# A hybrid decoder trunk in float32 on one core: the second low half of the first x block is queued without waiting for the low half of the weights

## Chip, cores and metric

The kernel runs on one core of one Trainium2 chip. The metric is the device time of one execution in microseconds (us). Lower is better.

## What is computed

The reference is a trunk with one attention layer and a final norm (the convolution layer has a weight of its own, but with a depth of one it is not reached). All of it is float32. Cut to what matters:

```python
D_MODEL = 4096; SEQ = 256; N_HEADS = 32; HEAD_DIM = 128
xn = rms_norm(x, norm_attn)                      # (256, 4096)
q, k, v, g = split(xn @ w_in_attn, 4)            # w_in_attn: (4096, 16384)
# strictly causal stick-breaking attention, head by head (log space, suffix sums)
A[t,s] = sigmoid(z_ts) * prod_{s<j<t} (1 - sigmoid(z_tj)),  s < t
o = A @ v
h = x + (o * silu(g)) @ w_out_attn               # w_out_attn: (4096, 4096)
return rms_norm(h, final_norm)
```

So there are two large products: 256 rows of x by a matrix of 4096 x 16384, and 256 rows of the gated heads by one of 4096 x 4096.

## The kernel before

**Products in three parts.** A float32 operand is split into a high part, which the tensor engine takes exactly (type fp32r), and a low part, the remainder. A product is then three matmuls that add up in one PSUM bank: high by high and two cross terms, in the names of the trace `wh,sh` (high weights, high x), `wl,sh` (low weights, high x) and `wh,sl` (high weights, low x). ScalarE (ACT) makes the high parts by a cast (`wh<-raw`), VectorE (DVE) the low ones by a subtraction (`wl<-raw,wh`). In the second large product the names of the left side are `oh` and `ol`.

**Units, steps and parts.** The work is a list of *units*: 16 over the columns of the first matrix (u = 0 to 15), then 4 over those of the second. A unit has 16 *steps* over the contracted dimension, and a step brings two tiles of weights (`raw`, 128 partitions by 1024 numbers, two transfers of 256 KB). In unit 0 a step is eight products, four on each tile, so 24 matmuls of 128x512; in the other units some steps get by with seven products, by sums and differences of blocks made on VectorE, and by an accumulating transfer on GpSimd's queue. Each unit writes PSUM banks b1 to b7. While unit u+1 multiplies, the attention of unit u's two heads runs between its matmuls. The very first tile of weights alone is cut into its two halves of 512 columns (c = 0 and 1), so that the first products can start earlier.

**x.** For unit 0 the left side comes from x transposed: step i takes block i, 256 columns of x by 256 rows, that is a pair of chunks c = 0 and 1 of 128 columns, each 128 partitions by 256 numbers. `blocks_of(i)` loads it (`xs`), multiplies it by the gain of the norm and makes the high and low parts (`sh`, `sl`). For i > 0 ACT scales and casts the whole pair. For i = 0 VectorE does it, chunk by chunk: `sh` of chunk c, then `sl` of chunk c. Afterwards the block is scaled in place on ACT (two ACTIVATEs) and differences of its quarters are made on VectorE, for the units that come later.

**What sets the order.** All engine work is emitted by a planner, class `Plan`, that runs a small event simulation while the program is built. Work is a set of generators. A generator asks for an engine (`nc.work`), waits for a name that another tells (`nc.until`, `nc.tell`), or takes a buffer of a ring (`nc.take`). When an engine of the simulation becomes free, the waiting request with the smallest key is emitted next: `key` is the time at which its product is due. What is emitted stays in that order on its engine (`keep_in_program_order`), and on the chip each engine takes its instructions in that order. The waits of the simulation are not waits on the chip: there an instruction waits only for the data and the buffers that it needs. So a line of the kernel that waits in the simulation moves instructions, and every later decision of the planner follows from the times of the earlier ones.

The places that the rest speaks of:

- `piece(n, c, ...)` makes high and low part of a tile or a half of one, and tells `("low", n, k)` once the low part of columns k is there. Part n = 0 is the first tile of step 0, n = 1 the second one, n = 2 and 3 the tiles of step 1, and so on.
- `products()` walks the list of products, and each asks for `("low", n, c)` and for the form of x that it uses.
- The last unit computes output columns 3072 to 4095 (blocks 6 and 7 of 512), as two row tiles t = 0 and 1. Its last five parts do their products bank by bank, `LAST_ORDER = (5, 4, 2, 3)`. Banks b5 and b4 complete row tile t = 1, and banks b2 and b3 complete t = 0. `block_done` adds a bank to `h`, `part_done` has ACT square and sum it, `finish` makes the factor of the final norm for all 128 rows of a tile, and `rows_out` scales the eight blocks of that tile and has SyncE (SP) issue their eight transfers to `out_dram`, 256 KB each.

Of the kernel before, what the change touches and what calls it, by code (L numbers as in the profile page):

```python
# [248 lines left out]
def kernel(  # L249
# [10 lines left out]
    nc = Plan(tc)  # L260
# [14 lines left out]
    def minus(out_, full, part):  # L275
        nc.vector.tensor_tensor(out=out_, in0=full, in1=part.bitcast(F32), op=ALU.subtract)
# [45 lines left out]
    def place_at(u, s):  # L322

        return place_of[u + int(s // NS), step_at(u + int(s // NS), int(s % NS))]
# [5 lines left out]
    def dve(emit, n, key=None, more=0, **kw):  # L330
        n = n if isinstance(n, tuple) else (n,)
        cost = sum(vector_ns(m) for m in n) + 122 * (len(n) - 1) + more
        return nc.work("vector", cost, emit, soon() if key is None else key, **kw)

    def act(emit, n, key=None, **kw):
        n = n if isinstance(n, tuple) else (n,)
        cost = sum(scalar_ns(m) for m in n) + 100 * (len(n) - 1)
        return nc.work("scalar", cost, emit, soon() if key is None else key, **kw)
# [14 lines left out]
    def moved(engine, emit, sizes, key, after=None, hold=False, adds=False, wait=0):  # L353
        issue = 550 if engine == "gpsimd" else 330
        return nc.work(
            engine, issue * len(sizes), emit, key, after=after, hold=hold, moves=[(4 * P * n, adds) for n in sizes],
            wait=wait,
        )
# [149 lines left out]
    def new_forms(i, what):  # L508
        n = len(SEVEN_FORMS if i in (SEVEN if what == "s" else SEVEN_OUT) else EIGHT_FORMS)
        h = sp.tile([P, n, P], F32R, tag=f"xh{i}", name=f"{what}h{i}")  # L510
        l = sp.tile([P, n, P], F32R, tag=f"xl{i}", name=f"{what}l{i}")
        forms[i] = h, l
        return h, l
# [18 lines left out]
    def sums_of(i, y, what, key):  # L532

        tt = nc.vector.tensor_tensor
        if i not in (SEVEN if what == "n" else SEVEN_OUT):
            yield from differences(i, y, key)
        else:

            def four():
                tt(out=y[:, 0, :], in0=y[:, 1, :], in1=y[:, 0, :], op=ALU.subtract)  # L540
                tt(out=y[:, 1, :], in0=y[:, 3, :], in1=y[:, 1, :], op=ALU.subtract)
                tt(out=y[:, 3, :], in0=y[:, 0, :], in1=y[:, 3, :], op=ALU.subtract)
                tt(out=y[:, 2, :], in0=y[:, 2, :], in1=y[:, 3, :], op=ALU.add)

            yield dve(four, (P, P, P, P), key)
            yield from both_parts(i, slice(4, 7), y[:, 1:4, :], key)

            yield nc.until(("used", 0 if what == "n" else OUT0, i))
            yield from both_parts(i, slice(1, 2), y[:, 0:1, :], key)
        nc.tell(("form", what, i))  # L550

    def blocks_of(i):

        key = place_of[0, i]
        tag = ("one", "two", "s", "s")[i % 4]
        yield nc.take(tag)
        pool, inside, bufs = (wp, "s", SINGLES) if tag == "s" else (ap, tag, 1)
        y = pool.tile([P, KT, S], F32, tag=inside, name=f"xs{i}", bufs=bufs)
        y4 = y.rearrange("p k (a b) -> p (k a) b", a=NT)
        h, l = new_forms(i, "s")  # L560
        gain = lambda c: gcol[:, i * KT + c : i * KT + c + 1]
        if i:
            yield moved(
                "sync", lambda: nc.sync.dma_start(y, xT[i]), [KT * S], key - 1, hold=True, wait=1300 * i - 600 if i < 4 else 0
            )

            def scaled():
                for c in range(KT):
                    nc.scalar.activation(y[:, c, :], y[:, c, :], AF.Copy, scale=gain(c))
                nc.scalar.copy(h[:, 0:4, :], y4)  # L570

            yield act(scaled, (S, S, 2 * S), key - 2e3)
            yield dve(lambda: minus(l[:, 0:4, :], y4, h[:, 0:4, :]), 2 * S, key)
        else:
            yield moved("scalar", lambda: nc.scalar.dma_start(gcol, gain_in), [KC], key - 1)
            yield moved("scalar", lambda: nc.scalar.dma_start(y, xT[i]), [KT * S], key - 1, hold=True)
            for c in range(KT):
                hc, lc = (t[:, 2 * c : 2 * c + 2, :].rearrange("p a b -> p (a b)") for t in (h, l))

                yield dve(  # L580
                    lambda: nc.vector.tensor_scalar(out=hc, in0=y[:, c, :], scalar1=gain(c), scalar2=None, op0=ALU.mult),
                    S, key - 1,
                )
                nc.tell(("sh", c))
                yield nc.until(("low", 0, c))
                yield dve(
                    lambda: nc.vector.scalar_tensor_tensor(
                        out=lc, in0=y[:, c, :], scalar=gain(c), in1=hc.bitcast(F32), op0=ALU.mult, op1=ALU.subtract
                    ),
                    S, key - 1,  # L590
                )
        nc.tell(("form", "s", i))
        later = place_at(0, i + BLOCKS_LATER)
        if not i:

            def scaled():
                for c in range(KT):
                    nc.scalar.activation(y[:, c, :], y[:, c, :], AF.Copy, scale=gain(c))

            yield act(scaled, (S, S), later)  # L600
        yield from sums_of(i, y4, "n", later)
        nc.give(tag)


    def blocks_all():
        for i in range(1, NS):
            if i > 3:
                yield nc.until(("used", 0, i - 4))
            nc.start(blocks_of(i))

    together(blocks_of(0), load(), blocks_all())
    nc.run(1e3)
    warm = att.tile([P, W], F32, tag="att", name="warm")
# [723 lines left out]
```

## Time and profile before

| | |
|---|---|
| time, median of 3 runs | 1693.47 us (1693.3 to 1694.87) |
| the profiled execution's own time | 1693.27 us |
| its span in the profile | 1691.6 us |
| busy share of the span | PE 99%, weight loads 84%, DVE 95%, ACT 71%, GpSimd 19% |
| granted TensorE clock | 0.997 |
| HBM read and written | 403 MB and 8 MB, 243 GB/s over the span |

The profile counts its times from the start of the span. PE is the tensor engine's matmuls, PEld its weight loads, DVE is VectorE, ACT is ScalarE, SPq is the queue of SyncE, which issues most transfers. A row of the timeline gives the start, the duration, engine, line and operation, out<-in, the shape and a count, and in square brackets how long the engine sat idle before it and what ended that. All instructions stand on L132, the line of the recording helper, so they are told apart by the names of their tiles. Matmuls overlap: one of 128x512 is listed with some 0.38 us, while the next starts 0.22 us after it.

### The profile page before, as it was taken

The page shows a single profiled execution, that of the slowest core. Times are in us where ns is not written, and L with a number is a line of the kernel's source. Part 1 is how long each engine was busy: PE and PEld are TensorE (multiplying, and loading weights), DVE is VectorE, ACT ScalarE, POOL GpSimd, SP SyncE. Part 2 cuts the span into 40 slices and gives each one's busy share as a digit, 9 for nine tenths or more (in the row PEclk, how much of TensorE's full clock was granted, in tenths as well). Part 3 has the DMA queues.
Part 4 walks back from the last instruction along what each step waited for, and adds up shares of the span by engine and source line. Part 5 has one row for each costly group of instructions (what it writes and reads, how often), then busy time and mean ns, then how long its engine had stood idle before and what let it go on. Part 6 is the DMA issues. An engine that isn't in the chain of part 4 may idle for free.

```text
span 1691.6 us, 25185 instructions
## 1 busy us (share of the span) xinstructions
PE 1674.7 (99%) x7776; PEld 1418.6 (84%) x7776; DVE 1600.5 (95%) x2025; ACT 1202.2 (71%) x1665; POOL 325.3 (19%) x400
## 2 busy tenths in 40 slices
PE   9999999999999999999999999999999999999996
PEld 7888888888888888888888888888888888888885
DVE  8889999999999999999999999999999977999997
ACT  8986767676767686867676767686867775666664
POOL 0012222222222221222222121212121111212110
PEclk9999999999999999999999999999999999999998
DMA  9978887878797978787979787978797877889895
GB/s 342 334 199 246 234 240 223 247 228 247 225 255 213 257 216 253 217 266 203 269 204 270 200 269 209 261 210 255 218 254 220 285 259 245 247 244 262 249 288 197
DMA packets 248440, 412.78 MB, mean 244 GB/s; under 512 B 28016, under 2 KB 72560, under 8 KB 248304
## 3 DMA queue, kind: packets, MB, share of 16 engines
q1 hardware_dynamic: 194544, 354.24, 62.4%
q0 software_dynamic: 53472, 56.65, 20.3%
q8 instruction: 61, 1.00, 0.2%
q14 instruction: 75, 0.61, 0.1%
q10 hardware_dynamic: 288, 0.28, 0.1%
HBM read 402.93 MB, written 8.13 MB: 243 GB/s over the span
## 4 chain that ended last, share of the span: by engine, by line
PE 96%; DVE 2%; DMA 1%; issue 1%; ACT 0%; SPq 0%; DVEq 0%; ACTq 0%
PE acc L132 91%; PE z L132 3%; PE o L132 1%; PE tr L132 1%; DVE wl L132 1%; DVE h L132 1%; DVE raw L132 0%; DMA raw<-in_w_in_dram 0%; DMA xres<-in_x_dram 0%; ACT wh L132 0%; DMA raw<-in_w_out_dram 0%; SPq L132 0%; DVE scalars L132 0%; ACT sq L132 0%; DVE wh L132 0%
## 5 line engine op out<-in xcount | busy, mean ns | idle before, releaser
L132 ACT CAST wh<-raw 128x1024 fp32r<-128x1024 f32 (+1 forms) x989 | 916.4, 969 | 364.1 <-DVE raw L132 162.2
L132 DVE TENSOR_TENSOR wl<-raw,wh 128x1024 fp32r<-128x1024 f32 (+1 forms) x815 | 968.9, 1217 | 45.9 <-ACT wh L132 24.7
L132 PE MATMUL acc<-wh,sh 128*128 128x512 f32 x2048 | 769.1, 387 | 0.0
L132 PE MATMUL acc<-wh,sl 128*128 128x512 f32 x1898 | 726.5, 383 | 1.7 <-DVE sl L132 1.7
L132 PE MATMUL acc<-wl,sh 128*128 128x512 f32 x1748 | 668.2, 382 | 0.0
L132 POOL DMA_DIRECT2D raw<-in_w_in_dram x300 | 258.7, 956 | 969.1 <-DMA raw<-in_w_in_dram 436.4
L132 PEld LDWEIGHTS acc<-wh,sh 128*128 128x128 f32 x2048 | 383.8, 188 | 69.3 <-ACT wh L132 0.8
L132 PEld LDWEIGHTS acc<-wh,sl 128*128 128x128 f32 x1898 | 355.6, 187 | 66.7 <-DVE sl L132 2.3
L132 PEld LDWEIGHTS acc<-wl,sh 128*128 128x128 f32 x1748 | 328.0, 188 | 56.9 <-DVE wl L132 0.4
L132 DVE TENSOR_TENSOR raw<-raw,raw 128x512 f32<-128x512 f32 x348 | 237.9, 684 | 3.5 <-DMA raw<-in_w_in_dram 1.7
L132 PE MATMUL acc<-wh,oh 128*128 128x512 f32 x512 | 192.1, 383 | 0.0
L132 PE MATMUL acc<-wh,ol 128*128 128x512 f32 x488 | 186.5, 382 | 0.0
L132 PE MATMUL acc<-wl,oh 128*128 128x512 f32 x464 | 177.3, 382 | 0.8 <-DVE wl L132 0.8
L132 DVE TENSOR_TENSOR wh<-raw,wh 128x512 fp32r<-128x512 f32 x174 | 118.8, 683 | 0.2
L132 DVE TENSOR_TENSOR raw<-raw 128x512 f32<-128x512 f32 x174 | 118.7, 682 | 0.0
L132 PEld LDWEIGHTS acc<-wh,oh 128*128 128x128 f32 x512 | 96.0, 187 | 17.1
L132 PEld LDWEIGHTS acc<-wh,ol 128*128 128x128 f32 x488 | 91.4, 187 | 16.1
L132 PEld LDWEIGHTS acc<-wl,oh 128*128 128x128 f32 x464 | 87.0, 187 | 16.7 <-DVE wl L132 1.4
L132 POOL DMA_DIRECT2D raw<-in_w_out_dram x48 | 41.6, 975 | 175.1 <-DMA raw<-in_w_out_dram 70.3
L132 ACT ACTIVATE f<-f 128x384 f32<-128x384 f32 x96 | 50.4, 525 | 3.0
L132 DVE SCALAR_TENSOR_TENSOR gv_sb<-acc,scalars,gv_sb 128x512 f32<-128x512 f32 x45 | 33.5, 745 | 0.4
L132 POOL DMA_DIRECT2D p<-spill x27 | 16.1, 660 | 88.9 <-DVE ol L132 44.6
(86 smaller groups left out, 765.6 us busy)
## 6 DMA issues: line engine op xcount, KB each, us to landing
raw<-in_w_in_dram SPq DMA_DIRECT2D x1024, 256.0 KB, 4.5
raw<-in_w_out_dram SPq DMA_DIRECT2D x256, 256.0 KB, 4.5
raw<-in_w_in_dram POOLq DMA_DIRECT2D x300, 128.0 KB, 5.2
p<-spill POOLq DMA_DIRECT2D x27, 256.0 KB, 4.7
raw<-in_w_out_dram POOLq DMA_DIRECT2D x48, 128.0 KB, 5.3
xr<-in_x_dram SPq DMA_DIRECT2D x16, 256.0 KB, 5.5
xres<-in_x_dram SPq DMA_DIRECT2D x16, 256.0 KB, 5.4
out_dram<-h SPq DMA_DIRECT2D x16, 256.0 KB, 2.9
```

The costliest lines, as they stand in the source:

```text
L132: return self.tc.keep_in_program_order(getattr(self.engine, name)(*args, **kw))
```

## The change

The generator for block 0 of x no longer waits, before it asks for the second chunk's low part, until the simulation has the low part of the weights' second half. For the first chunk it still does:

```diff
                 nc.tell(("sh", c))
-                yield nc.until(("low", 0, c))
+                if c == 0:
+                    yield nc.until(("low", 0, c))
                 yield dve(
                     lambda: nc.vector.scalar_tensor_tensor(
                         out=lc, in0=y[:, c, :], scalar=gain(c), in1=hc.bitcast(F32), op0=ALU.mult, op1=ALU.subtract
```

No instruction is added or removed. The order in which the planner emits them is another one, at the start and in many places behind it. A row of the lists below is an instruction: line, operation, out<-in and the shape of what it writes, with numbers of buffers in the names; - is the order before, + the order now.

The first place is VectorE, in step 0. `xs_78`, `sh_79` and `sl_80` are block 0 of x and its high and low parts, `wl_165` is the low part of the second half of tile n = 0, `wl_176` (now `wl_180`) that of tile n = 1, `sl_87` the low part of block 1 of x, `wl_202` (now `wl_215`) that of tile n = 2:

```order
 L132 TENSOR_SCALAR sh_79<-xs_78,gcol 128x256
+L132 SCALAR_TENSOR_TENSOR sl_80<-xs_78,gcol,sh_79 128x256
 L132 TENSOR_TENSOR wl_165<-raw_0_81,wh_159 128x512
-L132 TENSOR_TENSOR wl_176<-raw_1_95,wh_170 128x1024
-L132 SCALAR_TENSOR_TENSOR sl_80<-xs_78,gcol,sh_79 128x256
+L132 TENSOR_TENSOR wl_180<-raw_1_95,wh_170 128x1024
 L132 TENSOR_TENSOR sl_87<-xs_85,sh_86 128x512
+L132 TENSOR_TENSOR xs_78<-xs_78 128x2x128
 L132 TENSOR_TENSOR xs_85<-xs_85 128x128 x4
-L132 TENSOR_TENSOR wl_202<-raw_0_145,wh_182 128x1024
+L132 TENSOR_TENSOR wl_215<-raw_0_145,wh_194 128x1024
```

The low part of the second chunk moved ahead of two weight subtractions, and a difference of block 0 (`xs_78<-xs_78`) moved ahead of the subtraction for tile n = 2.

The second place is ACT at the same time. `wh_182` (now `wh_194`) is the high part of tile n = 2, the ACTIVATEs are the scalings of x:

```order
 L132 ACTIVATE xs_85<-xs_85,gcol 128x256 x2
 L132 CAST sh_86<-xs_85 128x512
-L132 CAST wh_182<-raw_0_145 128x1024
+L132 ACTIVATE xs_78<-xs_78,gcol 128x256 x2
+L132 CAST wh_194<-raw_0_145 128x1024
 L132 ACTIVATE xs_88<-xs_88,gcol 128x256 x2
 L132 CAST sh_89<-xs_88 128x512
-L132 ACTIVATE xs_78<-xs_78,gcol 128x256 x2
```

The two scalings of block 0 moved from behind the cast for tile n = 2 and block 2's work to ahead of that cast.

The third place is VectorE at the end of the program, after the last weights. `acc_3` is bank b3, which the last matmul of the program writes, and `h_0_15594` (now `h_0_15588`) is output block 7 of row tile t = 0. The four rows of `scalars` in the middle make the factor of row tile t = 1, and `h_1_13993`, `h_14701`, `h_15418` and `h_1_15420` are four of its output blocks:

```order
 L132 TENSOR_SCALAR scalars<-scalars 128x1
+L132 TENSOR_TENSOR h_0_15588<-acc_3_15526,h_0_15588 128x256 x2
 L132 SCALAR_TENSOR_TENSOR scalars<-squares_of_rows,scalars 128x1
 L132 SCALAR_TENSOR_TENSOR scalars<-scalars 128x1
 L132 TENSOR_SCALAR scalars<-scalars 128x1
 L132 TENSOR_TENSOR scalars<-scalars 128x1
+L132 SCALAR_TENSOR_TENSOR scalars<-squares_of_rows,scalars 128x1
 L132 TENSOR_SCALAR h_1_13993<-h_1_13993,scalars 128x512
 L132 TENSOR_SCALAR h_14701<-h_14701,scalars 128x512
 L132 TENSOR_SCALAR h_15418<-h_15418,scalars 128x512
 L132 TENSOR_SCALAR h_1_15420<-h_1_15420,scalars 128x512
-L132 TENSOR_TENSOR h_0_15594<-acc_3_15530,h_0_15594 128x256
```

Both additions of bank b3 moved from behind the factor and the scaled blocks of row tile t = 1 to ahead of them.

## The prediction

> **What bounds the kernel now.** I read the page first, then the list of what the tensor engine waited for, then the timeline at the two ends. The first row is the page's busy time, the other three are all that PE waited for in the whole span (engine, releaser, us in total, times, longest):
>
> ```profile
> PE 1674.7 (99%) x7776; PEld 1418.6 (84%) x7776; DVE 1600.5 (95%) x2025; ACT 1202.2 (71%) x1665; POOL 325.3 (19%) x400
> PE acc L132 <- DVE sl L132: 1.7, 1, 1.7
> PE warm L132 <- DVE idle L132: 1.3, 1, 1.3
> PE acc L132 <- DVE wl L132: 0.8, 1, 0.8
> ```
>
> PE is fed for the whole span but for three waits. So a gain can come from those few microseconds or from the stretches ahead of the first and behind the last matmul, and nothing in between has more to give. One wait is the change's target: 1.7 us for a low part of x (`sl`). Here it is on VectorE and on PE:
>
> ```profile
> 6.63 0.34 DVE L132 TENSOR_SCALAR sh<-xs,gcol 128x256 fp32r<-128x256 f32 x1
> 6.89 0.69 DVE L132 TENSOR_TENSOR wl<-raw,wh 128x512 fp32r<-128x512 f32 x1
> 8.37 1.22 DVE L132 TENSOR_TENSOR wl<-raw,wh 128x1024 fp32r<-128x1024 f32 x1 [0.79 <-ACT wh L132]
> 9.51 0.48 DVE L132 SCALAR_TENSOR_TENSOR sl<-xs,gcol,sh 128x256 fp32r<-128x256 f32 x1
> 9.91 0.68 DVE L132 TENSOR_TENSOR sl<-xs,sh 128x512 fp32r<-128x512 f32 x1
> 10.63 1.27 DVE L132 TENSOR_TENSOR xs<-xs 128x128 f32<-128x128 f32 x4
> 11.81 1.22 DVE L132 TENSOR_TENSOR wl<-raw,wh 128x1024 fp32r<-128x1024 f32 x1
> 13.55 1.60 DVE L132 TENSOR_TENSOR xs<-xs 128x256 f32<-128x256 f32 x5
> 15.07 1.22 DVE L132 TENSOR_TENSOR wl<-raw,wh 128x1024 fp32r<-128x1024 f32 x1
> ```
> ```profile
> 7.98 0.39 PE L132 MATMUL acc<-wl,sh 128*128 128x512 f32 x1
> 10.05 0.50 PE L132 MATMUL acc<-wh,sl 128*128 128x512 f32 x1 [1.68 <-DVE sl L132]
> 10.38 0.40 PE L132 MATMUL acc<-wh,sh 128*128 128x512 f32 x1
> ...
> 12.06 0.38 PE L132 MATMUL acc<-wl,sh 128*128 128x512 f32 x1
> ...
> 14.13 0.39 PE L132 MATMUL acc<-wl,sh 128*128 128x512 f32 x1
> ...
> 16.56 0.38 PE L132 MATMUL acc<-wh,sh 128*128 128x512 f32 x1
> ```
>
> The `sl` of the second chunk stood behind the low part of tile n = 1, whose cast came late (0.79 us idle). PE's eighth matmul started at 7.98 and the ninth at 10.05, where 0.22 is the usual distance: 1.85 us lost.
>
> **The change at the start.** The `sl` moves to 6.89. It takes 0.40 to the next start (9.51 to 9.91), so the weights' second half runs from 7.29 to 7.98 and the eighth matmul slips by 0.06, to 8.04. The ninth no longer waits. What is late next? The low part of n = 1 does not move: its cast sets it, 8.37 to 9.59. Matmul 14 is the first to need it. At 0.22 each it would start at 9.36 and waits to 9.65. Then n = 2, first needed by matmul 26 (14.13 before; it would now be 12.29). Here the order has put two scalings of block 0 on ACT, and its difference on VectorE, ahead of that tile:
>
> ```profile
> 9.17 0.62 ACT L132 CAST sh<-xs 128x512 fp32r<-128x512 f32 x1
> 9.70 1.04 ACT L132 CAST wh<-raw 128x1024 fp32r<-128x1024 f32 x1
> 10.64 0.90 ACT L132 ACTIVATE xs<-xs,gcol 128x256 f32<-128x256 f32 x2
> 11.58 0.62 ACT L132 CAST sh<-xs 128x512 fp32r<-128x512 f32 x1
> ...
> 16.27 0.81 ACT L132 CAST sh<-xs 128x256 fp32r<-128x256 f32 x2
> ```
>
> A pair of scalings takes 0.94 from start to start (10.64 to 11.58), so they run from 9.70 to 10.60, and the cast of n = 2 ends at 11.68, not 10.74. VectorE makes block 1's `sl` from 9.83, waits for the scalings and does the difference from 10.64 (0.34 to the next start: the five of row 13.55 take 1.52 to 15.07, four of them 1.18 as in row 10.63), the four small ones from 10.98 (1.18), and the low part of n = 2 from 12.16 to 13.38. Matmul 26 starts at 13.44 instead of 14.13: of 1.85 us some 0.7 is left. The tile after it, n = 3, follows from 14.13 to 15.35 by the same count (sh cast from 12.52, the tile's cast from 13.05 to 14.09) and is needed at about 16.3, so no further wait arises.
>
> Then the pitch. After the wait the matmuls came 0.24 apart (seven from 10.38 to 12.06) and the first one 0.33 behind, before they were back at 0.22 (eleven from 14.13 to 16.56): a wait cost 0.25 more than its length. If the new wait at matmul 26 costs the same, 0.45 us of gain is left at matmul 37. I take -0.45. The bounds are -2.1 (1.85 and the 0.25, if PE waits for nothing new) and +0.85 (in the rivals).
>
> The Trainium skill, "TensorE: Matmul & The Clock Gate", in its Part 1 on the clock gate, holds that only an idle window of about 3.4 us drops the clock; by that rule a wait of 1 to 2 us costs its length alone and the gain would be 0.7. The rows at 0.24 speak against it, so I keep 0.45.
>
> **Between the ends.** The order shifts the low and high parts of nearly every tile by nothing or by a few rows, and PE has one wait there, 0.8 us in the last units, where the subtractions ahead of the tile waited for are the same set as before. I take 0. The bounds are one row of 128x1024 either way, 1.2 us (row 8.37), and the 0.8 if that wait goes.
>
> **The change at the end.** This is where I expect the price. The last matmul of the program, the VectorE rows behind it, and the output transfers:
>
> ```profile
> 1678.05 0.40 PE L132 MATMUL acc<-wh,ol 128*128 128x512 f32 x1
> ```
> ```profile
> 1674.51 0.69 DVE L132 TENSOR_TENSOR h<-acc,h 128x512 f32<-128x512 f32 x1 [0.34 <-PE acc L132]
> 1676.31 0.15 DVE L132 SCALAR_TENSOR_TENSOR scalars<-squares_of_rows,scalars 128x1 f32<-128x1 f32 x1
> 1677.21 1.68 DVE L132 TENSOR_SCALAR h<-h,scalars 128x512 f32<-128x512 f32 x4
> 1678.80 0.42 DVE L132 TENSOR_TENSOR h<-acc,h 128x256 f32<-128x256 f32 x1
> 1679.14 0.74 DVE L132 SCALAR_TENSOR_TENSOR h<-h,scalars,grow 128x512 f32<-128x512 f32 x1
> 1679.80 0.42 DVE L132 TENSOR_TENSOR h<-acc,h 128x256 f32<-128x256 f32 x1
> 1682.05 1.28 DVE L132 TENSOR_SCALAR h<-h,scalars 128x512 f32<-128x512 f32 x3
> ```
> ```profile
> 1677.73 10.23 SPq L132 DMA_DIRECT2D out_dram<-h  x16
> 1678.00:1680.00 2.00, 0.44 (x2) 0.02 (x1) 2.00 (x6) 1.06 (x3) 0.00 (x0) 1.00 0.72 268
> 1680.00:1682.00 2.00, 0.00 (x0) 0.00 (x0) 0.96 (x6) 1.01 (x4) 0.00 (x0) 1.00 1.02 380
> 1682.00:1684.00 2.00, 0.00 (x0) 0.00 (x0) 1.96 (x6) 1.95 (x3) 0.00 (x0) 0.50 1.01 377
> 1684.00:1686.00 2.00, 0.00 (x0) 0.00 (x0) 1.32 (x2) 0.00 (x0) 0.00 (x0) 0.50 1.03 384
> 1686.00:1688.00 2.00, 0.00 (x0) 0.00 (x0) 0.00 (x0) 0.00 (x0) 0.00 (x0) 0.50 1.02 382
> 1688.00:1690.00 2.00, 0.00 (x0) 0.00 (x0) 0.00 (x0) 0.00 (x0) 0.00 (x0) 0.50 0.83 310
> ```
>
> These seven rows are SP's issue of the 16 outputs and busy time by stretch (the last two columns are the DMA engines' share and GB/s). While PE still multiplied for t = 0, VectorE made the factor of t = 1 (from 1676.31), scaled its blocks (1677.21), and the first output was issued at 1677.73. From 1680 to 1688 the DMA engines are full at 377 to 384 GB/s, VectorE's last rows or not. So the end is a train of 16 transfers, 4.19 MB, 11.0 us at 381 GB/s, and its start sets its end.
>
> Now both additions of b3 stand ahead of the factor of t = 1, and VectorE takes its instructions in order. They wait for the last matmul: 1678.05 + 0.40, and 0.06 to hand over (9.99 to 10.05 above), so 1678.51. Two additions at 0.34 (1678.80 to 1679.14) give 1679.19, the factor 0.90 (1676.31 to 1677.21), one more small row about 0.2, so the blocks of t = 1 start at 1680.29 instead of 1677.21: the train starts 3.1 us later against the last matmul. Is the rest in time? Four blocks take 1.59 (1677.21 to 1678.80), the factor of t = 0 another 0.90, the block with `grow` 0.66 (1679.14 to 1679.80): t = 0 follows from some 1683.4, when less than half of the train is through. I take +3.1. If the train could go as fast as its blocks are made, only VectorE's own delay would count. Before, the block of t = 0 that starts first did so at 1682.05, so that is 1.4 us, the lower bound.
>
> ```profile
> GB/s 342 334 199 246 234 240 223 247 228 247 225 255 213 257 216 253 217 266 203 269 204 270 200 269 209 261 210 255 218 254 220 285 259 245 247 244 262 249 288 197
> ```
>
> The upper bound is 4.3: at 342 GB/s, the most that one of the page's 40 slices moved (the row above), the train takes 12.3 us instead of 11.0.
>
> **Sum.** -0.45 + 0 + 3.1 = +2.65 us on the profiled execution's 1693.27: 1695.9. That execution is 0.2 under the median of the three, so against 1693.47 it is +0.14%. A measurement of this kernel tells about 0.2%, 3.4 us, from no change.
>
> **Rivals.**
> - *ACT pays for the start (slower).* The scalings and the cast of block 0's differences stand ahead of tiles that PE is about to need: 0.94 and, by half of the row at 16.27, 0.4 on ACT. VectorE has little slack there: n = 3 was ready at 16.29 (15.07 + 1.22) and PE took it at 16.78, one matmul behind the row at 16.56. If all 1.3 us lands on PE on top of my count, the start costs 0.85 instead of saving 0.45, and the sum is +3.95: 1697.2. With 3.1 for the end it crosses 0.2% once the start costs 0.5, so from 0.95 us on. For it: the chain of n = 2 already runs through ACT. Against: by my count n = 3 has almost 1 us to spare.
> - *The train goes slower (slower).* With all 16 blocks queued behind each other and no pause at the start, the train falls to a lower pace; half of the way from 381 to 342 GB/s adds 0.6, so +3.25: 1696.5. The Trainium skill, "DMA: Bandwidth & Descriptors", section "Where 436 GB/s comes from", puts the limit of transfers between HBM and SBUF at about 358 GB/s, which is about that pace. Against it: 377 to 384 GB/s for 8 us in the rows above. They are over the skill's figure, and they decide.
> - *The end costs nothing.* If the planner's order at the end were hidden, for example by outputs that wait for t = 0 anyway, only the start is left: -0.45, at best -2.1, so 1692.8 to 1691.2. For it: seven blocks of t = 1 are less than half of the train. Against it: the full DMA engines from 1680 on.
> - *The change does not do what it says.* The low part could stay late for another reason. The order shows it moved, and its inputs (`xs`, `sh`) are there at 6.97, so this has no chance of its own.
>
> **How the numbers follow.** My forecast 0.55, with an own range from 1694.9 (start -0.7, end 2.3, half of the way to its lower bound) to 1697.0 (start 0, end 3.7, half of the way to the upper one); ACT pays 0.25; slower train 0.10; the end costs nothing 0.10. Slower by over 0.2% is over 1696.9: 0.08 of the forecast, 0.21 of the first rival, 0.05 of the second, and 0.02 for a wait between the ends that adds to the forecast, together 0.36. Faster by over 0.2% is under 1690.1, beyond all bounds: 0.03. The rest, 0.61, is within 0.2%. The range leaves out 2 in 10: from 1693.6, with the third rival below it, to 1697.8, with 0.1 of the first and of a wait between the ends above it.
>
> **What would show it.** In the profile after: no wait for `sl` on PE, a wait of about 1.1 us for `wl` near 12.3 and one of 0.3 near 9.4, the first step's end 0.45 earlier; the span from the last matmul to the end 3.1 longer, with `h<-acc` 128x256 x2 ahead of the factor of t = 1, and the first `out_dram` issue some 2.8 behind the last matmul, not ahead of it. Wrong would be: the outputs start before the last matmul, or PE waits for weights anywhere from 20 to 1550.

## The result, and the profile after

| | before | after |
|---|---|---|
| median | 1693.6 us (18 runs) | 1697.91 us (18 runs) |
| ratio after / before | | 1.0022, 95% interval 1.0015 to 1.0028 |
| the profiled execution: time, span | 1693.27, 1691.6 us | 1698.33, 1696.6 us |

The ratio is an estimate of its own over these executions, and not quite that of the medians. It puts the change at +3.7 us (2.5 to 4.7). The two profiled executions are 5.06 us apart, and their rows say where. First the page's busy time and all that PE waited for (engine, releaser, us in total, times, longest), after:

```profile
PE 1677.0 (99%) x7776; PEld 1418.2 (84%) x7776; DVE 1607.4 (95%) x2025; ACT 1204.0 (71%) x1665; POOL 325.2 (19%) x400
PE acc L132 <- DVE wl L132: 1.9, 4, 0.8
PE warm L132 <- DVE idle L132: 1.3, 1, 1.3
PE acc L132 <- ACT wh L132: 0.5, 1, 0.5
```

The wait for `sl` is gone, and there are four waits for `wl` (1.9 us) instead of one (0.8). PE was busy 2.3 us longer with the same 7776 matmuls. The timeline of PE at the start, after: the first matmul on weights, matmul 26, matmul 37 and matmul 62.

```profile
5.50 0.46 PE L132 MATMUL acc<-wh,sh 128*128 128x512 f32 x1 [0.52 <-ACT wh L132]
...
13.28 0.49 PE L132 MATMUL acc<-wl,sh 128*128 128x512 f32 x1 [0.79 <-DVE wl L132]
15.82 0.38 PE L132 MATMUL acc<-wh,sh 128*128 128x512 f32 x1
...
21.33 0.38 PE L132 MATMUL acc<-wl,sh 128*128 128x512 f32 x1
```

Matmul 26 waits for the low part of n = 2, at 13.28 where the count said 13.44. Matmul 37 starts at 15.82 instead of 16.56, so 0.74 sooner, of which 0.25 is the first matmul's own (5.50; it was 5.75 before). At matmul 62, at 21.33 instead of 22.06, it is still 0.73.

The first head's transposes (`tr`) open the attention in each unit. A row of the tile view gives the shortest, median and longest of the four in ns, and when the first and the last of them started. Here they are in units 3 and 15, before and then after:

```profile
L132 PE MATMUL tr<-ident,qk_sb x4: 272/273/274, 260.5 to 260.8; 128*128 128x128 f32 x4
L132 PE MATMUL tr<-ident,qk_sb x4: 272/272/274, 1264.9 to 1265.3; 128*128 128x128 f32 x4
```
```profile
L132 PE MATMUL tr<-ident,qk_sb x4: 272/272/274, 259.7 to 260.1; 128*128 128x128 f32 x4
L132 PE MATMUL tr<-ident,qk_sb x4: 272/273/274, 1266.1 to 1266.5; 128*128 128x128 f32 x4
```

At 260 the changed kernel is 0.8 ahead, at 1265 it is 1.2 behind. PE waits for nothing in that stretch, and still each of the twelve units between these rows takes 83.87 us instead of 83.71: 2.0 us without a wait.

Next, unit 18: VectorE waited for a block of the residual (`xres`), and PE for the tiles behind it. After, VectorE's row and then PE's:

```profile
1566.53 0.69 DVE L132 TENSOR_TENSOR h<-h,xres 128x512 f32<-128x512 f32 x1 [0.95 <-DMA xres<-in_x_dram]
...
1571.35 0.50 PE L132 MATMUL acc<-wl,oh 128*128 128x512 f32 x1 [0.41 <-DVE wl L132]
...
1577.16 0.50 PE L132 MATMUL acc<-wl,oh 128*128 128x512 f32 x1 [0.48 <-DVE wl L132]
```

Before, VectorE did not wait for `xres` here, and PE waited once, for 0.8. From the transposes at 1266.1 to the last matmul at 1680.45 the changed kernel took 414.35 us, and before it was 413.15 (1264.9 to 1678.05): another 1.2. Of this, 0.9 lies in the 150 matmuls around these waits (35.06 us instead of 34.17). Last, the end, after: the last matmul, VectorE's additions of bank b3 and the scaled blocks of t = 1, SP's issue of the outputs, and two of the stretches of 2 us.

```profile
1680.45 0.40 PE L132 MATMUL acc<-wh,ol 128*128 128x512 f32 x1
1680.89 0.75 DVE L132 TENSOR_TENSOR h<-acc,h 128x256 f32<-128x256 f32 x2 [1.58 <-PE acc L132]
1682.45 1.67 DVE L132 TENSOR_SCALAR h<-h,scalars 128x512 f32<-128x512 f32 x4
1682.97 9.97 SPq L132 DMA_DIRECT2D out_dram<-h  x16
1684.00:1686.00 2.00, 0.00 (x0) 0.00 (x0) 1.82 (x8) 1.26 (x3) 0.00 (x0) 0.50 1.03 379
1690.00:1692.00 2.00, 0.00 (x0) 0.00 (x0) 0.00 (x0) 0.00 (x0) 0.00 (x0) 0.50 1.03 384
```

The outputs start 2.52 behind the last matmul, not 0.32 ahead of it, and the train runs at 379 to 384 GB/s as before. From the last matmul to the end of the span it is 16.18 us instead of 13.52: +2.66.

So -0.74 + 2.0 + 1.2 + 2.66 = 5.1. The experiments ask which of these belong to the change.

### The profile page after: what moved, and what is told of

Its sections match the earlier page's. It is cut to its first block, busy times and chain, and to the rows that moved or that the text cites. A ratio compares the mean times of both kernels' runs of the same rounds, so it can differ in the third digit from the quotient of the medians.

```text
span 1696.6 us, 25190 instructions
## 1 busy us (share of the span) xinstructions
PE 1677.0 (99%) x7776; PEld 1418.2 (84%) x7776; DVE 1607.4 (95%) x2025; ACT 1204.0 (71%) x1665; POOL 325.2 (19%) x400
## 4 chain that ended last, share of the span: by engine, by line
PE 96%; DVE 2%; DMA 1%; issue 0%; ACT 0%; SPq 0%; DVEq 0%; ACTq 0%
PE acc L132 91%; PE z L132 3%; PE o L132 1%; PE tr L132 1%; DVE wl L132 1%; DMA xres<-in_x_dram 1%; DVE h L132 0%; DVE raw L132 0%; DMA raw<-in_w_in_dram 0%; SPq L132 0%; ACT wh L132 0%; ACT xs L132 0%; DVE scalars L132 0%; DVE xs L132 0%; DVE wh L132 0%
## 5 line engine op out<-in xcount | busy, mean ns | idle before, releaser
L132 ACT ACTIVATE a<-z 128x384 f32<-128x384 f32 x32 | 15.7, 491 | 25.8 <-PE z L132 25.0
```

The source lines that it names most:

```text
L132: return self.tc.keep_in_program_order(getattr(self.engine, name)(*args, **kw))
```

## The experiments

Each of the first four moves one thing. Times are medians; ratios stand against the kernel before on the same chip.

### The start alone

VectorE makes the second `sl` right behind its `sh`; every other row stays where before has it.

```diff
-                yield dve(lambda: nc.vector.tensor_scalar(out=hc, ...), S, key - 1)
+                def high():
+                    nc.vector.tensor_scalar(out=hc, ...)
+                    if c == 1:
+                        low()
...
+                yield dve(high, S, key - 1)
                 nc.tell(("sh", c))
                 yield nc.until(("low", 0, c))
-                yield dve(lambda: nc.vector.scalar_tensor_tensor(out=lc, ...), S, key - 1)
+                yield dve(low if c == 0 else (lambda: None), S, key - 1)
```

> The kernel before with one row moved: the low part of the second chunk stands behind its high part on VectorE, every other row of every engine stays where it was (the two scalings of block 0 stay behind the cast for tile n = 2). Theory: the change at its place is worth the whole wait of 1.85 us, less about 0.3 at the tile n = 1, and the scalings that moved with it in the changed kernel cost what is missing there (1.18 at n = 2). So -1.5 us, between -1.2 and -2.1, no wait for wl near 12, no change behind the first step. Rival, the start's gain is lost further on because something else sets the pace there: -0.5 or nothing, with a new wait before 100 us. Rival, the middle's 2 us in the changed kernel come from PE being early: then this kernel drifts as the changed one did and is slower than before by about 0.5.

1694.83 us against 1694.65, ratio 0.9999 (0.9991 to 1.0007): the gain of 1.5 did not come. PE's timeline, first matmul, matmul 38 and matmul 62; below it matmul 62 of the kernel before:

```profile
5.93 0.46 PE L132 MATMUL acc<-wh,sh 128*128 128x512 f32 x1 [0.79 <-DVE sh L132]
16.13 0.50 PE L132 MATMUL acc<-wl,sh 128*128 128x512 f32 x1 [0.21 <-DVE wl L132]
21.70 0.38 PE L132 MATMUL acc<-wl,sh 128*128 128x512 f32 x1
```
```profile
22.06 0.38 PE L132 MATMUL acc<-wl,sh 128*128 128x512 f32 x1
```

Matmul 38 now waits for the tile n = 3: the wait only moved on, as the rival had it. From the first matmul to the 62nd it is 15.77 us, before 16.31. Half a microsecond, then, and even that is in doubt: the next experiment has the start of before and takes less. The profiled execution then lost 1.27 us at one place, in unit 8 (84.98 instead of 83.71). ACT's rows and the transposes there, and ACT at the same place in the changed kernel:

```profile
676.71 0.62 ACT L132 CAST wh<-raw 128x512 fp32r<-128x512 f32 x1 [0.44 <-DMA raw<-in_w_in_dram]
678.16 0.72 ACT L132 ACTIVATE qk_sb<-gv_sb,scalars 128x512 f32<-128x512 f32 x1 [0.83 <-DVE gv_sb L132]
680.10 0.55 PE L132 MATMUL tr<-ident,qk_sb 128*128 128x128 f32 x3 [0.93 <-DVE qk_sb L132]
```
```profile
676.08 0.73 ACT L132 ACTIVATE qk_sb<-gv_sb,scalars 128x512 f32<-128x512 f32 x1 [2.31 <-DVE gv_sb L132]
```

In the order of before, a cast that waits for a transfer stands close ahead of the work for `qk_sb`, and when that transfer is late, PE waits at the transposes. In the changed order it does not stand there. Four of the five profiles with the order of before in the units have one to three such waits in units 3 to 15 (the kernel before itself none), and none of the seven with the changed order. Over the five they cost 1.1 us on average.

### The end alone, in both directions

In the kernel before, the factor of t = 1 waits until the planner has emitted b3's additions:

```diff
+        if b == 3:                      # block_done, behind its additions
+            nc.tell("C21")
...
+        if t:                           # finish, ahead of the factor
+            yield nc.until("C21")
         yield dve(factor, (1, 1, 1, 1), late - 2)
```

> The kernel before with the end's order of the changed kernel: both additions of bank b3 stand ahead of the factor of row tile t = 1 on VectorE, nothing ahead of the last ten microseconds moves. Theory: the outputs start behind the last matmul instead of ahead of it and the train sets the end: +2.7 us (from the last matmul to the end 13.5 becomes 16.2), between 2.3 and 3.1. Rival, what the changed kernel lost at its end came from its earlier delays: 0 to +1.

1697.23 us, ratio 1.0013 (1.0005 to 1.0021): +2.2 us (0.8 to 3.6). Its first matmul, the wait for `sl` and matmul 62; then the last matmul, the additions and SP's issue:

```profile
5.65 0.46 PE L132 MATMUL acc<-wh,sh 128*128 128x512 f32 x1 [0.56 <-ACT wh L132]
9.38 0.50 PE L132 MATMUL acc<-wh,sl 128*128 128x512 f32 x1 [1.07 <-DVE sl L132]
21.33 0.38 PE L132 MATMUL acc<-wl,sh 128*128 128x512 f32 x1
```
```profile
1678.16 0.40 PE L132 MATMUL acc<-wh,ol 128*128 128x512 f32 x1
1678.59 0.76 DVE L132 TENSOR_TENSOR h<-acc,h 128x256 f32<-128x256 f32 x2 [2.09 <-PE acc L132]
1680.67 10.36 SPq L132 DMA_DIRECT2D out_dram<-h  x16
```

The end (to the span's 1694.6) is 16.48, so +2.96 by these two additions alone. And the start of before, unchanged, waits 1.07 here and takes 15.68 from the first matmul to the 62nd. How long that wait is depends on when the tile n = 1 lands; here its cast, on ACT, starts at 6.61 behind a wait of 0.59, and in the profile of before it had waited twice as long:

```profile
7.28 1.05 ACT L132 CAST wh<-raw 128x1024 fp32r<-128x1024 f32 x1 [1.17 <-DMA raw<-in_w_in_dram]
```

In the changed kernel, the additions go behind the scaled blocks of t = 1 again:

```diff
         for k, cut in enumerate(cuts):
-            yield add(h[:, cut], bank[b][:, cut], h[:, cut], late - 2, cut.stop - cut.start)
+            if b == 3:
+                yield nc.until(("factor", 1))
+            yield add(h[:, cut], bank[b][:, cut], h[:, cut], late + 105.5 + k if b == 3 else late - 2, ...)
```

> The changed kernel with the end's order of before: the additions of bank b3 stand behind the scaled blocks of t = 1 again, nothing else moves. Theory: -2.7 us against the changed kernel, so about +1.9 against the kernel before (the middle's +2.0 and +1.1, the start's -0.5 to -0.7). Rival, the end costs nothing by itself: no difference from the changed kernel, +4.6 against before.

1695.51 us, ratio 1.0004 (0.9996 to 1.0013), so about 3 us better than the changed kernel, and +0.7 us (-0.7 to 2.2) against the kernel before, where +1.9 was expected. Its last matmul and SP's issue, and its transposes in unit 15:

```profile
1679.71 0.40 PE L132 MATMUL acc<-wh,ol 128*128 128x512 f32 x1
1680.12 9.99 SPq L132 DMA_DIRECT2D out_dram<-h  x16
```
```profile
L132 PE MATMUL tr<-ident,qk_sb x4: 272/273/274, 1266.5 to 1266.9; 128*128 128x128 f32 x4
```

The end is 14.1 (span 1693.8), 2.1 less, not 2.7: the outputs now start 0.41 behind the last matmul, where before had them 0.32 ahead, since the changed order also has the rest of t = 1 later. So of the 2.66, 2.1 is the additions and 0.6 the order ahead of them. The other 1.2 of the changed kernel did not come back here: with the same order in unit 18, this execution needs 413.2 us from the transposes to the last matmul, as the kernel before does. So its size changes from execution to execution. The exposure comes with the order, though. In the changed order VectorE comes to this block of `xres` about 5 us sooner, and in six of the seven profiles with that order it waits there for 0.33 to 0.95 us (0.08 in the seventh); in none of the five with the order of before does it wait. In time the two are not apart: the stretch takes 412.8 to 414.3 us in six profiles with the changed order (mean 413.7; the seventh runs at another pace, as below) and 412.9 to 414.0 in the five with the order of before (mean 413.2). How much of the 1.2 belongs to the change stays open.

### The scores of the second head

The small matmuls of the attention come in bursts between the large ones of 128x512: transposes, then scores (`z<-qkT`), then products with v (`o`). In the changed kernel the scores of the second head follow six large matmuls behind that head's transposes; before, nine. This emits them one product later, with every other engine's rows in order:

```diff
-        yield ten(scores, *FULL_P, *FULL_S, 2 * P)
+        if i == 1 and 1 < u < NS - 1:
+            yield nc.work("tensor", ..., lambda: held.append(scores), nc.here - 1e4, wait=400)
+        else:
+            yield ten(scores, *FULL_P, *FULL_S, 2 * P)
...
             orders,
         )
+        if held:                        # product, behind its three matmuls
+            held.pop()()
+            since_others = 0
```

> The changed kernel with one group moved on PE: in units 3 to 15 the scores of the second head (five matmuls into z) follow one product later, so nine matmuls stand between them and that head's transposes, as before, instead of six. Rows of the other engines stay in order. Theory: the drift of 0.16 us in each of these 13 units is the price of two bursts of small matmuls so close together, as a run of matmuls at 0.225 to 0.24 follows the second burst: -1.9 us against the changed kernel, between -1.4 and -2.2, so about +2.7 against before. Rival, the drift comes from elsewhere in the unit (the nine instead of twelve matmuls between the heads, weights that arrive later, or this one execution): 0 to -0.5 against the changed kernel.

1693.98 us, ratio 0.9995 (0.9987 to 1.0004). Its transposes in units 3 and 15:

```profile
L132 PE MATMUL tr<-ident,qk_sb x4: 272/272/274, 260.4 to 260.7; 128*128 128x128 f32 x4
L132 PE MATMUL tr<-ident,qk_sb x4: 269/272/273, 1263.4 to 1263.8; 128*128 128x128 f32 x4
```

1003.0 us instead of 1006.4 over twelve units: the place is right, but the gain of 3.4 is nearly twice what was expected, and more than the 2.0 that the change had cost there. The matmuls of the first head, which nothing had moved, had become faster too: the run of large matmuls behind its scores went from 0.29 over its plain pace of 0.22 a matmul to 0.13. Counted as the first 22 distances, from start to start, of the large matmuls behind the scores, the second head's run went from 5.12 us to 4.99 and the first head's from 5.12 to 4.95, together 0.30 a unit. In unit 3, where the first head's scores still come ahead of the first ones that were moved, its run takes 5.12 here too: the move shows in the unit behind it.

### Distance or moment

The same edit for the first head (`i == 0 and u < NS - 1`) in the kernel before:

> The kernel before with the scores of every first head one product later on PE (nine matmuls between that head's transposes and its scores, as before's second head has, instead of six); rows of the other engines stay in order. In the kernel before, the run of matmuls behind the first head's scores took 0.29 us over its plain pace and that behind the second head's 0.16. Theory, the distance of the two bursts sets which: 0.13 us in each of 15 units, -2.0 us, between -1.5 and -2.3. Rival, such a run has a short and a long form and the moment at which the burst begins picks one, whatever the distance (in the changed kernel with the second scores later, the first head's run went to 0.13 although its six matmuls stayed): the units change by another amount, from -2 to +2, and the second head's run may go to its long form.

1693.95 us, ratio 0.9999 (0.999 to 1.0008): no gain to be seen. The run behind the scores did go from 0.29 over its plain pace to 0.15, but the nine matmuls ahead of them took 0.16 instead of 0.12 for six, and a unit is 83.61 instead of 83.71. That is 1.5 us in all, which three waits for `qk_sb` at the transposes took back in the profiled execution.

The other two pieces undone together (the end and the second head's scores, in the changed kernel):

> The changed kernel with two of its side effects undone: the end's order of before, and the scores of the second head one product later. The order of the first steps stays that of the change. Theory, the parts add up: the end -2.7 and the units -3.6, as each measured by itself, so -6.2 us against the profiled execution of the changed kernel: 1692.1, that is about -1.5 against the kernel before, between -0.5 and -2.2. Rival, the start or the middle holds more of the loss (the wait for the residual at unit 18): no better than the kernel before.

1692.0 us, ratio 0.9985 (0.9977 to 0.9994): 2.5 us under the kernel before (1.0 to 3.9), where -1.5 was expected, and the lowest ratio of all. The expected -6.2 against the changed kernel came out as about -6.3 by the two ratios. Its transposes, and all of PE's waits:

```profile
L132 PE MATMUL tr<-ident,qk_sb x4: 272/273/274, 260.1 to 260.5; 128*128 128x128 f32 x4
L132 PE MATMUL tr<-ident,qk_sb x4: 269/272/272, 1263.2 to 1263.5; 128*128 128x128 f32 x4
```
```profile
PE warm L132 <- DVE idle L132: 1.3, 1, 1.3
PE acc L132 <- DVE wl L132: 1.1, 2, 0.9
PE acc L132 <- DVE sh L132: 0.2, 1, 0.2
```

With the first heads' scores later as well:

> The run before this one with the first heads' scores one product later as well. Theory of the distance: the first head's run is in its short form there already, so nothing changes, within 0.5 us. Rival, the moment of the burst: one of the runs changes its form, up to +2 us.

1692.45 us, ratio 0.999 (0.9981 to 0.9998), and 83.60 instead of 83.57 us a unit: nothing gained, as the theory of the distance had it.

Then an edit that moves nothing: in the changed kernel, the seventh product behind a burst writes its columns in runs of eight throughout (`e`), instead of two of its matmuls in runs of four (`c`).

```diff
-BEHIND_OTHERS = ("ccc", "ecc", "eee", "eee", "eee", "eee", "cce")
+BEHIND_OTHERS = ("ccc", "ecc", "eee", "eee", "eee", "eee", "eee")
```

> The changed kernel with the order in which one product's matmuls write their columns changed: the seventh product behind every burst of small matmuls writes in runs of eight throughout, instead of two matmuls in runs of four. No instruction is added, removed or moved; the distance between the bursts stays six matmuls. In the changed kernel's rows such a pair takes 0.013 us over its pace, and there are up to three per unit. Theory of the moment: a few nanoseconds at the burst decide between the short form (0.13 to 0.16) and the long one (0.29 to 0.30) of the run behind the scores, so one of the two runs of a unit changes its form, 0.15 us a unit, some 2 us in all. Theory of the distance: both stay long, and a unit is shorter by 0.02 to 0.05 alone, 0.3 to 0.8 us in all.

1697.79 us, ratio 1.0022 (1.0013 to 1.0032). The first matmul behind the first head's scores in unit 10 and the 23rd, in the changed kernel and then here; below, the transposes of units 3, 4 and 5 here:

```profile
849.28 0.48 PE L132 MATMUL acc<-wh,sh 128*128 128x512 f32 x1
854.40 0.38 PE L132 MATMUL acc<-wl,sh 128*128 128x512 f32 x1
```
```profile
849.82 0.47 PE L132 MATMUL acc<-wh,sh 128*128 128x512 f32 x1
854.77 0.38 PE L132 MATMUL acc<-wl,sh 128*128 128x512 f32 x1
```
```profile
L132 PE MATMUL tr<-ident,qk_sb x4: 272/273/275, 259.9 to 260.2; 128*128 128x128 f32 x4
L132 PE MATMUL tr<-ident,qk_sb x4: 270/272/273, 344.1 to 344.4; 128*128 128x128 f32 x4
L132 PE MATMUL tr<-ident,qk_sb x4: 273/273/275, 427.6 to 428.0; 128*128 128x128 f32 x4
```

22 distances take 5.12 us in the one and 4.95 in the other, six matmuls after the transposes in both. So at this distance a run has a long and a short form. But the next unit goes the other way: units take 83.56 and 84.20 in turn, 167.76 the pair where the changed kernel has 167.74, so what one unit gains its neighbour loses. The expected 2 us in all did not come.

The order of the matmuls does not pick the form either. In the changed kernel units 2 and 3 have the same 392 matmuls in the same order, with the same columns, and take 83.56 and 83.87. In the first experiment unit 9, behind the late `qk_sb` of unit 8, takes 83.55, and unit 10 with the same matmuls 83.71. So it is something that one unit hands on to the next, such as the moment at which a run begins; no run here tells which. The distance does count all the same: with nine matmuls between a head's transposes and its scores the 22 distances take 4.98 to 5.00 in each of the 137 cases in units 2 to 15 of the twelve profiles, and with six 4.95 to 5.13 in 199 cases. Nine gives one form, six leaves it open.

The same edit at the first product of each step (`IN_STEP = ("eee", "eee")`):

> The changed kernel with the same edit at another place: the first product of every step writes its columns in runs of eight throughout, instead of two matmuls in runs of four. No instruction is added, removed or moved. Of the pairs that are taken out three or four in a unit took 0.013 us over their pace. Theory of the moment: the forms of the runs behind the scores change here too, by 0.15 us a unit and run, up or down. Theory of the distance: both stay long (0.29 to 0.30), and a unit is shorter by 0.03 to 0.06, 0.5 to 1 us in all.

1699.68 us, ratio 1.003 (1.0018 to 1.0041). Units 4 to 15 take 83.50 us, 0.37 less than in the changed kernel, but before the first attention it loses 3.6 (0.4 of it ahead of the first matmul), and behind the transposes of unit 15 another 1.8. PE in the stretch from 30 to 60 us (busy, matmuls, granted clock, DMA share, GB/s), here and in the changed kernel:

```profile
30.00:60.00 30.00, 30.00 (x131) 1.00 0.97 338
```
```profile
30.00:60.00 30.00, 30.00 (x138) 1.00 0.96 337
```

131 matmuls instead of 138 with PE busy throughout and the clock at 1.00 in both: a distance of 0.229 instead of 0.217. It holds for as long as no burst interrupts it, and it is back in the last 300 matmuls of the program, which run 0.231 apart instead of 0.220.

### What the start waits for

The start alone, with block 0's scalings put behind the cast of n = 3 and its difference behind that tile's low part:

```diff
-            yield act(scaled, (S, S), later)
+            yield act(nc.behind("scalar", 1, scaled), (S, S), later)
...
-        yield dve(minus_, 2 * P, key)
+        yield dve(nc.behind("vector", 2, minus_) if y is first_block.get("y") else minus_, 2 * P, key)
```

> The first experiment (only the low part of the second chunk moved) with the scalings of block 0 on ACT and its difference on VectorE put behind the cast and the low part of tile n = 3. Theory: what limited the first experiment's start was the supply, ACT without a gap from 7.1 us on, so that matmul 38 waited for n = 3 at 16.13; now that tile is ready at 15.75 instead of 16.07 and the wait of 0.39 at matmul 38 shrinks to 0.1 or goes, with its slower matmuls behind it: -0.4 to -0.6 us at matmul 62 against the first experiment, counted from the first matmul. Rival, the next tile is then late by as much: no difference at matmul 62.

First matmul, matmul 38 and matmul 62:

```profile
6.07 0.57 PE L132 MATMUL acc<-wh,sh 128*128 128x512 f32 x1 [0.29 <-DVE sh L132]
15.74 0.49 PE L132 MATMUL acc<-wl,sh 128*128 128x512 f32 x1
21.27 0.38 PE L132 MATMUL acc<-wl,sh 128*128 128x512 f32 x1
```

15.20 us from the first matmul to the 62nd, 0.57 less than without, as expected, and the wait for n = 3 at matmul 38 is gone, though it still started 0.29 late. That fits a start bound by ACT's and VectorE's supply. One profile of each does not show it: three profiles with the same start, that of before, lie up to 0.6 apart. In the time it does not show (1694.75 us, ratio 1.0002, 0.9993 to 1.0011); the profiled execution had two late `qk_sb` of 0.3 and 1.3 us.

## Why the prediction was right, and where it was not

- **The whole.** 1695.9 was forecast, 2.4 us over the median of the three runs. The ratio says +3.7, on that median 1697.2: in the range, 0.2 above the forecast's own, and above the line of 0.2%, to which the prediction gave 0.36; the interval from 0.15 to 0.28% does not settle on which side of the line the change lies.
- **Start, -0.45.** Its steps held but for one: no wait for `sl`, matmul 26 at 13.28 (13.44 forecast), no wait at n = 3; 0.74 sooner at matmul 37, 0.49 without the earlier first matmul. The wait of 0.3 at matmul 14 did not come: it started at 9.49 (9.65 forecast), 0.09 late. But the base was one execution. By the rows of matmuls 1 and 62, three profiles with the start of before take 15.68 to 16.31 us, and five with the changed start and its columns as they were 15.74 to 16.39. Their means are 0.1 apart, within the scatter. The rival that ACT pays did not occur.
- **Pitch behind a wait.** PE in the stretch of the matmuls at 0.24, before (busy, matmuls, granted clock, DMA share, GB/s):

```profile
10.00:12.00 2.00, 1.95 (x8) 1.00 1.05 402
```

  The clock was 1.00. So the rule of the Trainium skill, "TensorE: Matmul & The Clock Gate", Part 1, that only an idle window of about 3.4 us drops the clock, agrees with the trace. The prediction took the rows at 0.24 as evidence against it; they were a slow pace at full clock, as the last section has it. The size of 0.25 did not carry over: behind the wait at matmul 26 of the changed kernel one distance was 0.33, one 0.23 and the nine after them 0.22, so the wait cost 0.12 over its length.
- **Between the ends, 0.** This step failed. The argument was that PE waits for nothing there, so nothing can change. PE did wait for nothing, and 2.0 us came from its own pace: the planner had fallen into another periodic order, with six matmuls instead of nine ahead of the second head's scores, and from unit 3 on the 22 distances behind them took 5.12 instead of 4.99. The bounds of 1.2 were bounds of a wait, not of this. Moving the second head's scores removed it. Why stays open, since with the same order they took 4.99 in unit 2.
- **End, +3.1.** The mechanism is shown from both sides: the two additions cost 2.96 in the kernel before and, taken out again, 2.1 in the changed one, where another 0.6 came from the order ahead of them. In the changed kernel the whole end was 2.66: the blocks of t = 1 started 2.00 behind the last matmul (2.24 forecast), and the train took 0.18 less. That the train would be slower is out: 379 to 384 GB/s. That the end costs nothing is out too.
- **What would have shown it wrong** did not occur: no output before the last matmul, no wait for weights from 20 to 1550. Of its signs, the wait near 12.3 was 0.79 (1.1 forecast) and the first output came 2.52 behind the last matmul (2.8).

Start -0.1, units +2.0 and end +2.7 make +4.6, near the upper end of the interval from 2.5 to 4.7. What is likely to lower it are the late `qk_sb` that the changed order spares, 1.1 us on average in five profiles; how often they occur in executions without a profile was not measured. So that the whole came out in the range is in part luck: by these terms it would have been 1698.1, above the range, and a loss that the kernel before shows in some profiles is likely to have brought it back.

## What to carry to other kernels

Where a scheduler follows from simulated times, an edit at the start is an edit of everything behind it: price the last instructions before the outputs, and allow the busy engine's own pace some tenths of a microsecond per repeated unit even where it waits for nothing. An in-order engine must not stand at a wait for the very last product while work for half of the outputs is ready behind it. A wait at the start that depends on when a transfer lands should be taken from several profiles, and its gain counted only up to the next tile that the supplying engines can have ready.

## What the hardware showed

- At full granted clock and without a wait, matmuls of 128x512 run at two paces, 0.22 and about 0.23 us. Behind a burst of small matmuls they run at the slower one for a while, and how long hangs on more than the instructions and their order: 22 distances of 5.12 or 4.95 us behind the same burst, alternating units of 83.56 and 84.20, units of 83.56 and 83.87 with the same 392 matmuls. Without bursts the slower pace held through unit 0 where the first product of each step wrote its columns in runs of eight throughout (131 matmuls in 30 us from 30 us on; 138 where two of its matmuls wrote in runs of four). In units 4 to 15 the same runs of eight made a unit 0.37 us shorter. What causes it stays open, and so does whether the other engines' work at the same moment has a part in it; no run here shows that.
- A wait can leave the slower pace behind it, but need not: seven distances of 0.24 behind the wait of 1.68 us in the kernel before, one of 0.33 and one of 0.23 behind the wait of 0.79 in the changed one, at a clock of 1.00.
- The same order repeats to 0.01 us a unit from execution to execution, except where a transfer lands late and in the unit or two behind that. One late tile of weights cost up to 1.3 us, where a cast that waits for it stands close ahead of the work that the transposes need.
